# Attention heads in pairs and in a written order, with projections between their steps

## The chip, the cores and the metric

One Trainium2 chip, one NeuronCore of it. The time is device time in microseconds of one execution; a kernel's time is the median of several runs. All times of the trace count from the span's start.

The engines are TensorE (PE; PEld are its weight loads), VectorE (DVE), ScalarE (ACT), GpSimd (POOL) and SyncE (SP), which issues DMAs.

## The reference

Two models stand one behind the other on one sequence of 256 tokens, d_model 1024, all in float32.

The first has two layers on the sequence `x` and a context of 256 tokens `xc`, with modulated norms: a SwiGLU (`ffn1`, d_ff 2816), a mixer of gated convolution, pooling over four windows and neighbourhood attention (eight heads of 64; in layer 0 the context's own attention too), an output projection, and a second SwiGLU. The second has two layers (`hybrid_layer`): one input projection feeds sliding-window attention with sinks (A), stick-breaking attention (B) and block attention (C), each with eight heads of 64; three gated branches are merged, and a SwiGLU with a causal convolution follows.

```
def rms_norm(x, g):
    xf = x.astype(jnp.float32)
    y = xf * lax.rsqrt(jnp.mean(xf * xf, axis=-1, keepdims=True) + RMS_EPS)
    return (y * g.astype(jnp.float32)).astype(x.dtype)

def mod_norm(x, m, i, g):
    return rms_norm(x, g) * (1 + m[:, 3 * i + 1, None]) + m[:, 3 * i, None]
...
        s = jnp.concatenate([s_loc.reshape(B, NA_HEADS, nj, NA_QC, n_loc), s_ctx], axis=-1)
        p = jax.nn.softmax(s, axis=-1).astype(v.dtype)
...
        remain = lax.cumsum(log_one_minus, axis=3, reverse=True) - log_one_minus
        w = jnp.where(past, jnp.exp(log_beta + remain), 0.0)
        return jnp.einsum('bhqk,bkhd->bqhd', w.astype(v.dtype), v)
```

## The kernel before

Activations lie transposed, 128 channels by tokens, in eight tiles (`KT`) for 1024 channels; `n` is 512 where both sequences go through a stage, else 256. A projection (`project`, L149) multiplies weights of a chunk (256 columns by 1024 rows, loaded by `weights`, L109) with these tiles. Each product of float32 operands is done as three products of high and low parts (`mm3`, L139); `split` (L105) makes the parts: ScalarE copies the high part (L106), VectorE subtracts it for the low part (L107). The matmul proper is L133, for projections; in a page its operands are `whi`/`wlo` (weights) and `hhi`/`hlo`, `xhi`/`xlo`, `xg`, `h`, `ghi`/`glo` (activations).

`stats` (L198) gives the root mean square of the normalisation: squares on ScalarE and sums on VectorE (L168), column sums by TensorE with `ones` (`sums`, L178), the power on POOL (L186, `rsqrt`), and `spread` (L189), which turns the four columns by TensorE to all partitions (L193) and copies them (L195). The pair `(0, 0)` says at which `tick` of the projections the two steps come: a tick comes after half of a projection and at its end. A few products on the unnormalised tiles `xhi`/`xlo` run meanwhile; `normed` (L239) then makes the normalised tiles, with a product, an affine operation and a split.

`mix1` (L637) is the mixer of layers 0 and 1. It projects all queries, keys and values, then runs the heads in pairs, with two queries' halves a pair (`attn1`, L601): scores of both heads (L612), softmax on VectorE and ScalarE, transposition of the weights by TensorE (`pt`, L633), values (`o`, L710). Each head has 64 channels, so its scores run on half of the array's rows and its values on half of its columns. The masks of a pair of heads (`bias1`, L593) come by a DMA of POOL's queue and are subtracted on POOL (L598). The gated convolution and the pooling are projected between and after the pairs.

`layer2` (L903) does the same in two layers: the chunks of A, B and C are projected, each group followed by its four pairs of heads (`pair2` L778, `softmax2` L787, `stick2` L808, `pv2` L830; scores L784, transposes L802, stick-breaking sums L821 to L824, values L834 and L836); then twelve chunks of gates, the branches and the ffn.

What sets the order: except where `self.chain` is set, a scheduler puts ready instructions of each engine in an order of its own, and queues and pools of tiles bound what is ready. `mm` (L131) chains matmuls one behind the other only with `self.chain` on. The attentions' matmuls don't go through `mm`, and are not chained.

Of the kernel before, what the change touches and what calls it, by code (L numbers as in the profile page):

```python
# [16 lines left out]
KT = 8  # L17
# [7 lines left out]
WINDOWS = (2, 4, 8, 16)  # L25

# [29 lines left out]
class Kernel:  # L56
# [17 lines left out]
    def chunks():  # L74
# [6 lines left out]
        def mix(l):  # L81
            return [("w_in", l, c) for c in (4, 5, 6, 7, 8, 9, 3, 2, 0, 1)] + [("w_out", l, c) for c in range(4)]
# [48 lines left out]
    def mm(self, *a, **k):  # L131

        i = self.nc.tensor.matmul(*a, **k)  # L133
        if self.chain:
            if self.chained is not None:
                self.after(i, self.chained)
            self.chained = i

# [10 lines left out]
    def project(self, w, width, cols, ops, n):  # L149
        banks = [self.bank("mm") for _ in cols]  # L150
        k = len(ops)
        for i in range(k):
            for ps, c in zip(banks, cols):
                self.mm3(ps[:, :n], self.w_at(w, i, width, c), ops[i], i == 0, i == k - 1)
            if i in (k // 2 - 1, k - 1):
                self.tick()
        return banks

    def project_tok(self, w, width, c0, ops, tts):
        banks = [self.bank("mm") for _ in tts]  # L160
        k = len(ops)
        for ps, tt in zip(banks, tts):
            for i in range(k):
                a = tuple(o[:, tt * 128:tt * 128 + 128] for o in ops[i])
                self.mm3(ps[:, :256], a, self.w_at(w, i, width, c0, 256), i == 0, i == k - 1)
        return banks
# [55 lines left out]
    def modnorm(self, l, i, n, nd):  # L222
# [370 lines left out]
    def bias1(self, l, h):  # L593
        nc = self.nc
        a = self.act(name="tb")
        tb = a[:, :384].rearrange("p (a b) -> p a b", b=64)
        self.after(nc.gpsimd.dma_start(tb, self.t["rpb"][l, h]), self.power)
# [3 lines left out]
    def attn1(self, q, k, tbs):  # L601
# [5 lines left out]
        pts = [self.ptp.tile([128, 4, 256], F32, tag="ptw", name="ptw") for _ in range(2)]  # L607
        for qt in range(2):
            scs = [self.bank("sc") for _ in range(2)]
            for a, sc in enumerate(scs):  # L610
                r = slice(64 * a, 64 * a + 64)
                nc.tensor.matmul(sc[:, :nk], q[r, c0 + qt * 128:c0 + qt * 128 + 128], k[r, c0:c0 + nk], start=True, stop=True)  # L612
            for a, sc in enumerate(scs):
                s = self.swp.tile([128, 512], F32, tag="s", name="s")
                nmx = self.sp.tile([128, 2], F32, tag="nmx", name="nmx")
                if ctx:
                    nc.vector.tensor_reduce(nmx[:, 1:2], sc[:, :256], axis=AX.X, op=ALU.min)
                    ss = self.sp.tile([128, 1], F32, tag="ss", name="ss")
                    self.tabled(nc.scalar.activation(s[:, :256], sc[:, :256], AF.Exp, bias=nmx[:, 1:2], scale=-1.0, accum_out=ss))
                    nc.vector.reciprocal(ss, ss)  # L620
                    nc.vector.tensor_scalar_mul(s[:, :256], s[:, :256], ss)
                else:
                    e0 = 2 - 2 * qt
                    nc.vector.tensor_tensor_reduce(
                        out=s[:, :256], in0=sc[:, :256], in1=tbs[a][0][:, e0:e0 + 4, :].rearrange("p a b -> p (a b)"), scale=1.0, scalar=HUGE,
                        op0=ALU.add, op1=ALU.min, accum_out=nmx[:, 0:1])
                    nc.vector.tensor_tensor_reduce(
                        out=s[:, 256:], in0=sc[:, 256:], in1=self.zeros.to_broadcast([128, 256]), scale=1.0, scalar=nmx[:, 0:1],
                        op0=ALU.add, op1=ALU.min, accum_out=nmx[:, 1:2])
                    self.softmax_tail(s, 512, nmx[:, 1:2])  # L630
                pp = self.bank("pt")
                for kt in range(nk // 128):
                    nc.tensor.transpose(pp[:, kt * 128:kt * 128 + 128], s[:, kt * 128:kt * 128 + 128], self.ident)  # L633
                nc.scalar.activation(pts[a][:, :nk // 128, qt * 128:qt * 128 + 128], pp[:, :nk].rearrange("p (k q) -> p k q", q=128), AF.Copy)
        return pts

    def mix1(self, l, fill=()):  # L637
# [25 lines left out]
        if not last:  # L663
            for ps in self.project(self.weights("w_in", l, 5), 256, (0, 128), sl(n1), n1):
                q = self.act(name="q")
                nc.scalar.activation(q[:, :n1], ps[:, :n1], AF.Copy, scale=-0.125)
                Q.append(q)
        for c in (6, 7):
            for ps in self.project(self.weights("w_in", l, c), 256, (0, 128), sl(512), 512):
# [3 lines left out]
        for c in (8, 9):  # L673
            w = self.weights("w_in", l, c)
            for tt, ps in enumerate(self.project_tok(w, 256, 0, ops, range(4))):
                nc.scalar.activation(V[tt][:, (c - 8) * 256:(c - 8) * 256 + 256], ps[:, :256], AF.Copy)

        def sums(m):
            v, su3 = Z[m]
            self.pool_sums(v, ns, m, su3)  # L680
            nc.gpsimd.tensor_tensor(su3, su3, self.invcnt[:, m, None, :].to_broadcast([128, ns, 256]), op=ALU.mult)
            nc.gpsimd.tensor_tensor(su3, su3, v[:, :ns, 8:264], op=ALU.subtract)

        tbs = [[self.bias1(l, h) for h in range(2)]]
        SU, Z = [], []
        for m, ps in enumerate(self.project(self.weights("w_in", l, 3), 256, (0, 128), sl(n1), n1)):
            v = self.zp.tile([128, 2, 272], F32, tag="z", name="z")
            nc.gpsimd.memset(v[:, :, 0:8], 0.0)
            nc.gpsimd.memset(v[:, :, 264:272], 0.0)
            nc.scalar.activation(v[:, :ns, 8:264], ps[:, :n1].rearrange("p (s t) -> p s t", t=256), AF.Copy)  # L690
# [212 lines left out]
    def layer2(self, L):  # L903
# [68 lines left out]
        if L == 0:  # L972
            close()
# [294 lines left out]
```

## Time and profile before

| | us |
|---|---|
| median of 3 runs | 2617.03 (2615.76 to 2618.78) |
| profiled execution | 2616.04 |
| its span | 2614.3 |
| PE busy | 2576.7 (99%) |
| DVE busy | 1761.1 (67%) |
| ACT busy | 1172.8 (45%) |
| POOL busy | 72.1 (3%) |

The span is the time from the first to the last instruction of the core. A busy share says in how much of it the engine worked, not whether what it did was needed or at the best rate: a TensorE that computes one half of its array at a time is busy all the same. The chain of work that ended last has TensorE in 78% of it, with the projections' L133 alone 72%.

Timelines list start and duration of groups of equal instructions of one line. One float32 matmul of attention makes two records, a transposition one; a projection's matmul of split operands makes one. Times of matmuls' ends are modelled, so the steps between starts are the better measure of pace.

### The profile page before, as it was taken

How to read it: one execution, taken by the hardware profiler on the slowest of the kernel's cores; microseconds unless marked ns; L12 is line 12 of the kernel's file. 1: busy time of each engine (PE TensorE's matmuls, PEld its weight loads, DVE VectorE, ACT ScalarE, POOL GpSimd, SP SyncE). 2: the span in 40 equal slices, each digit the busy share in tenths (PEclk: the TensorE clock that was granted, in tenths of full speed). 3: DMA queues.
4: the chain of work that ended last, by engine and by line, in shares of the span. 5: the costliest groups of instructions: out<-in, count | busy, mean ns of one | idle time of the engine just before them, and what ended most of it. 6: DMA issues, size and time to landing. Idle time of an engine off the chain costs nothing.

```text
span 2614.3 us, 39984 instructions
## 1 busy us (share of the span) xinstructions
PE 2576.7 (99%) x16156; PEld 2241.0 (86%) x16156; DVE 1761.1 (67%) x3309; ACT 1172.8 (45%) x2120; POOL 72.1 (3%) x93
## 2 busy tenths in 40 slices
PE   8999999999999999999999999999999999999998
PEld 5888888668888888888887799988999998899998
DVE  6877755557867758765354665677579856758984
ACT  5222234545222234222234554457556645755664
POOL 0000002200000000000003000000000000000000
PEclk9999999999999999999999999999999999999999
DMA  7545533112545533444233254632454463245544
GB/s 289 214 161 192 175 128 115 55 52 106 192 160 191 176 122 144 175 163 155 73 127 119 95 187 166 203 137 101 162 190 170 169 211 133 98 164 192 178 163 145
DMA packets 64857, 401.69 MB, mean 154 GB/s; under 512 B 7456, under 2 KB 7584, under 8 KB 26656
## 3 DMA queue, kind: packets, MB, share of 16 engines
q1 hardware_dynamic: 63360, 395.20, 42.9%
q0 software_dynamic: 1024, 3.15, 0.4%
q8 instruction: 127, 2.08, 0.3%
q10 hardware_dynamic: 288, 0.79, 0.1%
q14 instruction: 58, 0.48, 0.1%
HBM read 398.06 MB, written 1.05 MB: 153 GB/s over the span
## 4 chain that ended last, share of the span: by engine, by line
PE 78%; DVE 3%; ACT 2%; issue 1%; POOL 0%; POOLq 0%; DVEq 0%; ACTq 0%
PE mm L133 72%; PE sc L612 1%; PE sc L784 1%; PE o L834 1%; PE o L710 1%; PE pt L633 1%; DVE wlo L107 1%; ACT whi L106 1%; ACT t L845 1%; PE pt L802 1%; POOL r L186 0%; PE o L836 0%; PE pt L180 0%; DVE n L242 0%; PE sc L193 0%
## 5 line engine op out<-in xcount | busy, mean ns | idle before, releaser
L106 ACT ACTIVATE whi<-raw 128x1024 fp32r<-128x1024 f32 (+2 forms) x704 | 621.0, 925 | 545.0 <-issue 271.5
L107 DVE TENSOR_TENSOR wlo<-raw,whi 128x1024 fp32r<-128x1024 f32 (+2 forms) x704 | 730.4, 1066 | 166.2 <-ACT whi L106 165.2
L133 PE MATMUL mm<-hlo,whi 128*128 128x512 f32 (+1 forms) x1520 | 556.0, 366 | 2.9 <-DVE hlo L107 2.8
L133 PE MATMUL mm<-hhi,wlo 128*128 128x512 f32 (+1 forms) x1520 | 555.8, 366 | 0.1
L133 PE MATMUL mm<-hhi,whi 128*128 128x512 f32 (+1 forms) x1520 | 553.4, 366 | 0.0
L133 PEld LDWEIGHTS mm<-hlo,whi 128*128 128x128 f32 x1520 | 285.4, 188 | 55.8 <-DVE hlo L107 3.4
L133 PEld LDWEIGHTS mm<-hhi,whi 128*128 128x128 f32 x1520 | 285.6, 188 | 52.6 <-issue 2.3
L133 PEld LDWEIGHTS mm<-hhi,wlo 128*128 128x128 f32 x1520 | 285.5, 188 | 52.4 <-issue 2.2
L133 PE MATMUL mm<-xg,whi 128*128 128x256 f32 x1600 | 294.4, 284 | 0.0
L517 ACT ACTIVATE t<-mm 128x512 f32<-128x512 f32 (+1 forms) x82 | 44.9, 547 | 522.1 <-PE mm L133 522.1
L133 PEld LDWEIGHTS mm<-xg,whi 128*128 128x128 f32 x1600 | 246.4, 188 | 5.1 <-issue 4.2
L133 PE MATMUL mm<-h,whi 128*128 128x256 f32 x1280 | 227.4, 280 | 0.3
L133 PE MATMUL mm<-xg,wlo 128*128 128x256 f32 x800 | 227.2, 284 | 0.0
L133 PE MATMUL mm<-ghi,whi 128*128 128x512 f32 x528 | 208.1, 394 | 0.0
L133 PE MATMUL mm<-ghi,wlo 128*128 128x512 f32 x528 | 207.9, 394 | 0.0
L133 PE MATMUL mm<-glo,whi 128*128 128x512 f32 x528 | 207.9, 394 | 0.0
L133 PEld LDWEIGHTS mm<-h,whi 128*128 128x128 f32 x1280 | 196.1, 188 | 1.2 <-DVE h L107 1.1
L434 DVE CUSTOM_DVE_ANT_0 junk<-raw,cb,par 128x1024 bf16<-128x1024 f32 x128 | 164.0, 1281 | 48.4 <-DMA raw<-in_w_mod 48.4
L416 DVE SCALAR_TENSOR_TENSOR x<-mm,m,x 128x256 f32<-128x256 f32 x128 | 56.0, 479 | 191.6 <-PE mm L133 191.0
L133 PE MATMUL mm<-h,wlo 128*128 128x256 f32 x640 | 179.0, 280 | 0.0
L434 DVE CUSTOM_DVE_ANT_0 raw<-raw,cb,par 128x1024 f32<-128x1024 f32 x128 | 164.4, 1284 | 3.6
L133 PEld LDWEIGHTS mm<-xg,wlo 128*128 128x128 f32 x800 | 151.2, 189 | 4.6 <-issue 4.1
(269 smaller groups left out, 4041.7 us busy)
## 6 DMA issues: line engine op xcount, KB each, us to landing
raw<-in_ffn_w_in SPq DMA_DIRECT2D x86, 1024.0 KB, 4.8
raw<-in_w_in SPq DMA_DIRECT2D x74, 1024.0 KB, 4.8
raw<-in_w_mod SPq DMA_DIRECT2D x64, 1024.0 KB, 4.8
raw<-in_ffn_w_out SPq DMA_DIRECT2D x64, 704.0 KB, 4.1
raw<-in_w_up SPq DMA_DIRECT2D x44, 1024.0 KB, 4.8
raw<-in_w_down SPq DMA_DIRECT2D x32, 704.0 KB, 4.1
raw<-in_w_out SPq DMA_DIRECT2D x16, 1024.0 KB, 4.8
raw<-in_w_branch SPq DMA_DIRECT2D x12, 1024.0 KB, 4.8
```

The source lines that it names most:

```text
L106: self.nc.scalar.activation(hi, src, AF.Copy)
L107: self.nc.vector.tensor_sub(lo, src, hi.bitcast(F32))
L133: i = self.nc.tensor.matmul(*a, **k)
L416: self.nc.vector.scalar_tensor_tensor(out=self.X[m][:, c], in0=ps[:, c], scalar=self.mod(l, i, m, r), in1=self.X[m][:, c], op0=ALU.mult, o ...
L434: nc.vector.tensor_tensor_reduce(out=w if r else self.junk, in0=w, in1=self.cb[:, r, :], scale=1.0, scalar=self.par["b_mod"][:, c:c + 1], ...
L517: self.tabled(nc.scalar.activation(g[:, :n], pa[:, :n], AF.Silu))
L612: nc.tensor.matmul(sc[:, :nk], q[r, c0 + qt * 128:c0 + qt * 128 + 128], k[r, c0:c0 + nk], start=True, stop=True)
L633: nc.tensor.transpose(pp[:, kt * 128:kt * 128 + 128], s[:, kt * 128:kt * 128 + 128], self.ident)
L710: nc.tensor.matmul(o[64 * a:64 * a + 64, :256], v[:, h * 64:h * 64 + 64], pts[a][:, kt, :], start=(kt == 0), stop=(kt == len(vs) - 1), til ...
L784: self.nc.tensor.matmul(sc[:, o:o + n], a[r, ca:ca + 128], b[r, cb:cb + n], start=True, stop=True)
L802: nc.tensor.transpose(pp[:, (qt + i) * 128 if qt == 0 or i == 0 else 256:((qt + i) * 128 if qt == 0 or i == 0 else 256) + 128], s[:, a + i ...
L834: nc.tensor.matmul(o[64 * a:64 * a + 64, 0:256], v[0][:, cols[a]:cols[a] + 64], pts[a][:, 0:256], start=True, stop=False, tile_position=(0 ...
```

## The change

Attention is cut into units: two heads, and in `mix1` one half of the queries. A unit has three steps: scores, `weights` (transposes, or the stick-breaking sums), values. `weave` issues a unit's scores, then projections for a given time, the unit before's `weights`, more projections, that unit's values, and goes on. `ROOM1` and `ROOM2` hold the times; a projection reports its time as columns times products over 2200. The projections come from a generator (`stream`), in which the chunks' order is written; what isn't used up goes behind the units. While `written()` is on, all of TensorE's instructions are chained through `mm` and `flip`.

Beside it: `stats` of modulated norms and of layer 2's ffn spread at tick 2; `normed` makes each tile by two products with the root mean square, two high parts on ScalarE and two differences of 256 columns; masks are subtracted by VectorE (`masked1`), for the first pair of heads ahead of the units, later beside them; chunk order in `w_in`; `w_out` takes the mixer's parts in the order 4, 5, 6, 7, 2, 3, 0, 1; the ffn of layer 2 has three early chunks; pools of weights and of `rb` in part 2 have two tiles instead of three, scores have four.

```
+ROOM1 = (((3.6, 2.4), (2.2, 1.4)), ((3.3, 2.2),) * 2)
+ROOM2 = (4.6, 3.0)
...
-            return [("w_in", l, c) for c in (4, 5, 6, 7, 8, 9, 3, 2, 0, 1)] + [("w_out", l, c) for c in range(4)]
+            return [("w_in", l, c) for c in ((4, 6, 8, 5, 7, 9), (4, 5, 6, 8, 7, 9))[l] + (3, 2, 0, 1)] + [("w_out", l, c) for c in range(4)]
...
+    def flip(self, dst, src):
+        self.link(self.nc.tensor.transpose(dst, src, self.ident))
...
+    def fill(self, us):
+        self.owed += us
+        while self.owed > 0 and self.stream is not None:
+            try:
+                self.owed -= next(self.stream)
+            except StopIteration:
+                self.stream = None
+
+    def weave(self, units, stream, lead):
+        self.stream, self.owed = stream, 0.0
+        with self.written():
+            self.fill(lead)
+            for u in range(len(units) + 1):
+                if u < len(units):
+                    while not units[u].ready():
+                        self.fill(0.1 - self.owed)
+                    units[u].scores()
+                a, b = units[u - 1 if u else 0].room
+                self.fill(a)
+                if u:
+                    units[u - 1].weights()
+                    self.fill(b)
+                    units[u - 1].values()
+            self.fill(1e6)
...
-        self.stats(self.X, n, (0, 0))
+        self.stats(self.X, n, (0, 2))
...
-                nc.vector.tensor_tensor(t[:, :n], self.X[kt][:, :n], self.rb[:, :n], op=ALU.mult)
+                hi, lo = self.act(F32R, "hhi"), self.act(F32R, "hlo")
                 for r in segs:
                     c = slice(r * 256, r * 256 + 256)
-                    if r and kt % 2:
-                        nc.vector.tensor_scalar(t[:, c], t[:, c], self.mod(l, i + 1, kt, r), self.mod(l, i, kt, r), op0=ALU.mult, op1=ALU.add)
-                    else:
-                        nc.scalar.activation(t[:, c], t[:, c], AF.Identity, bias=self.mod(l, i, kt, r), scale=self.mod(l, i + 1, kt, r))
-                hi, lo = self.act(F32R, "hhi"), self.act(F32R, "hlo")
-                self.split(hi[:, :n], lo[:, :n], t[:, :n])
+                    sh = self.mod(l, i, kt, r)
+                    nc.vector.scalar_tensor_tensor(out=t[:, c], in0=self.X[kt][:, c], scalar=self.mod(l, i + 1, kt, r), in1=self.rb[:, c], op0=ALU.mult, op1=ALU.mult)
+                    nc.scalar.activation(hi[:, c], t[:, c], AF.Identity, bias=sh)
+                    nc.vector.scalar_tensor_tensor(out=lo[:, c], in0=t[:, c], scalar=sh, in1=hi[:, c].bitcast(F32), op0=ALU.add, op1=ALU.subtract)
...
-        nc.gpsimd.tensor_tensor(tb, self.colmask[:, None, :].to_broadcast([128, 6, 64]), tb, op=ALU.subtract)
+    def masked1(self, tb):
+        self.nc.vector.tensor_tensor(tb, self.colmask[:, None, :].to_broadcast([128, 6, 64]), tb, op=ALU.subtract)
...
+        self.weave([unit(p, ctx, qt) for p in range(4) for ctx in ((False,) if last else (False, True)) for qt in range(2)], stream(), 1.4)
...
+        self.weave([f(m) for f in (unit_a, unit_b, unit_c) for m in range(4)], stream(), 6.0)
...
-        self.stats(X, 256, (0, 0))
+        self.stats(X, 256, (0, 2))
```

Three places of the order, before (first fence of each) and after. TensorE in the mixer of layer 1 (`mm` projections, `sc` scores, `pt` transposes, `o` values), where the first pairs of heads begin, before:

```order
L612 MATMUL sc<-k,q 128x512
L633 MATMUL pt<-ident,s 128x128 x4
L612 MATMUL sc<-k,q 128x512
L633 MATMUL pt<-ident,s 128x128 x4
L612 MATMUL sc<-k,q 128x512
L633 MATMUL pt<-ident,s 128x128 x4
L612 MATMUL sc<-k,q 128x512
L633 MATMUL pt<-ident,s 128x128 x4
L710 MATMUL o<-ptw,v 64x256
```

And after, further along in the same attention:

```order
L138 MATMUL mm<-hhi,whi 128x256
L138 MATMUL mm<-hlo,whi 128x256
L138 MATMUL mm<-hhi,wlo 128x256
L138 MATMUL o<-ptw,v 64x256 x8
L138 MATMUL sc<-k,q 128x512 x2
L138 MATMUL mm<-hhi,whi 128x256
L138 MATMUL mm<-hlo,whi 128x256
L138 MATMUL mm<-hhi,wlo 128x256
```

Scores of single heads stood between transposes of others; now a pair's two scores stand together, behind all eight value matmuls of the unit before, and projections go between the steps.

TensorE in layer 2's first layer, among the units of C (`qk` queries and keys, `xg` the projections' tiles), before:

```order
L784 MATMUL sc<-qk 128x128
L802 MATMUL pt<-ident,s 128x128
L784 MATMUL sc<-qk 128x256
L133 MATMUL mm<-xg,whi 128x256
L802 MATMUL pt<-ident,s 128x128 x2
L133 MATMUL mm<-xg,whi 128x256
L834 MATMUL o<-ptw,v 64x256
L784 MATMUL sc<-qk 128x128
L784 MATMUL sc<-qk 128x256
L834 MATMUL o<-ptw,v 64x256
L836 MATMUL o<-ptw,v 64x128 x2
```

And after:

```order
L138 MATMUL mm<-xg,whi 128x256 x2
L138 MATMUL mm<-xg,wlo 128x256
L138 MATMUL o<-ptw,v 64x256 x2
L138 MATMUL o<-ptw,v 64x128 x2
L138 MATMUL sc<-qk 128x128 x2
L138 MATMUL sc<-qk 128x256 x2
L138 MATMUL mm<-xg,whi 128x256 x2
L138 MATMUL mm<-xg,wlo 128x256
```

Scores and values of one unit were cut by transposes of another and by single projections; now both heads' scores, and both heads' values, are whole groups.

TensorE at the start of the ffn behind the first mixer (`pt<-ones,t` the column sums, `sc<-ident,r` the spread), before:

```order
L180 MATMUL pt<-ones,t 128x1 x4
L133 MATMUL mm<-xhi,whi 128x258
L133 MATMUL mm<-xlo,whi 128x258
L133 MATMUL mm<-xhi,wlo 128x258
L133 MATMUL mm<-xhi,whi 128x258
L133 MATMUL mm<-xlo,whi 128x258
L133 MATMUL mm<-xhi,wlo 128x258
L133 MATMUL mm<-xhi,whi 128x258
L193 MATMUL sc<-ident,r 128x128 x4
```

And after:

```order
L237 MATMUL pt<-ones,t 128x1 x4
L138 MATMUL mm<-xhi,whi 128x258
L138 MATMUL mm<-xlo,whi 128x258
L138 MATMUL mm<-xhi,wlo 128x258
L138 MATMUL mm<-xhi,whi 128x258
L138 MATMUL mm<-xlo,whi 128x258
L138 MATMUL mm<-xhi,wlo 128x258
L138 MATMUL mm<-xhi,whi 128x258
L138 MATMUL mm<-xlo,whi 128x258
L138 MATMUL mm<-xhi,wlo 128x258
L250 MATMUL sc<-ident,r 128x128 x4
```

Seven products stood between the column sums and the spread; now there are nine.

## Rows read from the trace of the kernel before

**Rows 1.** Page, busy time (share of the span) and instructions of each engine.

```profile
PE 2576.7 (99%) x16156; PEld 2241.0 (86%) x16156; DVE 1761.1 (67%) x3309; ACT 1172.8 (45%) x2120; POOL 72.1 (3%) x93
```

**Rows 2.** Windows of projections: length; PE, PEld, DVE, ACT, POOL busy (records); clock, DMA, GB/s.

```profile
200.00:300.00 100.00, 100.00 (x433) 80.90 (x432) 77.73 (x117) 26.82 (x36) 0.00 (x0) 1.00 0.52 185
2000.00:2100.00 100.00, 100.00 (x851) 100.00 (x850) 79.52 (x137) 63.79 (x106) 0.00 (x0) 1.00 0.51 178
```

**Rows 3.** Windows with attention, projections of L133 alone.

```profile
480.00:546.00 66.00, 15.07 (x51) 8.39 (x50) 1.00 0.07 23
1424.00:1465.00 41.00, 7.51 (x51) 6.13 (x49) 1.00 0.18 61
1716.00:1840.00 124.00, 79.06 (x597) 72.72 (x596) 1.00 0.32 113
2171.00:2297.00 126.00, 79.69 (x605) 73.55 (x604) 1.00 0.32 113
```

**Rows 4.** Timeline, mixer 0, both heads' scores: start, us, line, shape.

```profile
480.42 0.39 PE L133 MATMUL mm<-hhi,wlo 128*128 128x512 f32 x1
480.74 1.13 PE L612 MATMUL sc<-k,q 64*128 64x512 f32 x4
481.80 0.50 PE L133 MATMUL mm<-hhi,whi 128*128 128x512 f32 x1
482.14 0.39 PE L133 MATMUL mm<-hlo,whi 128*128 128x512 f32 x1
```

**Rows 5.** Timeline, mixer 1, scores of one head alone.

```profile
1430.89 1.12 PE L612 MATMUL sc<-k,q 64*128 64x512 f32 x2
```

**Rows 6.** Timeline, mixer 1, values of one unit.

```profile
1455.06 0.65 PE L710 MATMUL o<-ptw,v 128*64 128x256 f32 x2
...
1456.65 1.94 PE L710 MATMUL o<-ptw,v 128*64 128x256 f32 x14
```

**Rows 7.** Timeline, mixer 0, eight transposes, and a context pair's scores.

```profile
505.16 1.10 PE L633 MATMUL pt<-ident,s 128*128 128x128 f32 x8
506.01 0.48 PE L133 MATMUL mm<-hlo,whi 128*128 128x512 f32 x1
...
507.89 0.77 PE L612 MATMUL sc<-k,q 64*128 64x256 f32 x4
```

**Rows 8.** Timeline, layer 2, scores of both heads of a unit.

```profile
1762.87 0.92 PE L784 MATMUL sc<-qk 64*128 64x256 f32 x8
1763.73 0.50 PE L133 MATMUL mm<-xg,whi 128*128 128x256 f32 x2
```

**Rows 9.** Window with attention in layer 2, all engines.

```profile
1716.00:1840.00 124.00, 121.69 (x901) 102.32 (x900) 84.28 (x249) 81.42 (x190) 0.00 (x0) 1.00 0.32 113
```

**Rows 10.** TensorE's waits: total us, times, longest.

```profile
PE sc L193 <- POOL r L186: 5.2, 8, 0.9
...
PE o L834 <- ACT ptw L827: 3.0, 3, 1.5
PE mm L133 <- DVE hlo L107: 2.8, 1, 2.8
...
PE mm L133 <- DVE mlo L107: 1.4, 2, 0.8
```

**Rows 11.** VectorE's operations by form: count, busy us, mean ns.

```profile
L107 DVE TENSOR_TENSOR hlo<-n,hhi 128x512 fp32r<-128x512 f32 x32 | 23.7, 760 | 0.0
L242 DVE TENSOR_TENSOR n<-x,rb 128x512 f32<-128x512 f32 x32 | 22.7, 735 | 0.0
...
L246 DVE TENSOR_SCALAR n<-n,m,m 128x256 f32<-128x256 f32 x16 | 7.9, 495 | 0.0
...
L398 DVE SCALAR_TENSOR_TENSOR hlo<-n,m,hhi 128x256 fp32r<-128x256 f32 x16 | 6.9, 479 | 0.0
```

**Rows 12.** Timeline, VectorE and POOL at mixer 1's masks.

```profile
1378.62 1.48 DVE L107 TENSOR_TENSOR hlo<-n,hhi 128x512 fp32r<-128x512 f32 x1
...
1374.24 5.30 POOL L598 TENSOR_TENSOR tb<-k,tb 128x384 f32<-128x384 f32 x4 [1.10 <-DMA tb<-in_rpb]
```

More of the change, by code (lines that the diff above doesn't have):

```diff
@@ L606, in attn1 @@
         c0 = 256 if ctx else 0
[L607 to L634, printed above, removed]
@@ L662, in mix1, with head @@
         normed()
[L663 to L669, printed above, removed]
+        def head(c):
+            banks = yield from self.projected(self.weights("w_in", l, c), 256, (0, 128), sl(512), 512)
+            for ps in banks:
                 k = self.act(name="k")
@@ new lines, in stream @@
+        def stream():
+            if not last:
+                banks = yield from self.projected(self.weights("w_in", l, 5), 256, (0, 128), sl(n1), n1)
+                for ps in banks:
+                    q = self.act(name="q")
+                    nc.scalar.activation(q[:, :n1], ps[:, :n1], AF.Copy, scale=-0.125)
+                    Q.append(q)
+            yield from head(7)
+            yield from toks(9)
+            yield from pooled()
+            yield from conv()
+        SU, mix = [], [None] * 8
@@ new lines, in mix1, with unit, scores, weights @@
+        pair = lambda: (self.act(F32R, "mhi"), self.act(F32R, "mlo"))
+        tbs = [[self.bias1(l, h) for h in range(2)]]
+        self.drain(head(6))
+        self.drain(toks(8))
+        for tb, _ in tbs[0]:
+            self.masked1(tb)
+        PT = {}
+        def unit(p, ctx, qt):
+            def scores():
+                if qt == 0 and not ctx and p < 3:
+                    tbs.append([self.bias1(l, 2 * p + 2 + a) for a in range(2)])
+                u.S = self.scores1(Q[p], K[p], None if ctx else tbs[p], qt)
+                if qt and not ctx:
+                    self.slots.free(*(a for _, a in tbs[p]))
+                    if p < 3:
+                        for tb, _ in tbs[p + 1]:
+                            self.masked1(tb)
+                if qt and ctx != last:
+                    self.slots.free(Q[p], K[p])
+            def weights():
+                if qt == 0:
+                    PT[p, ctx] = [self.ptp.tile([128, 4, 256], F32, tag="ptw", name="ptw") for _ in range(2)]
+                self.turned1(u.S, PT[p, ctx], 2 if ctx else 4, qt)
+            def values():
+                if qt == 0:
+                    return
+                if not ctx:
+                    mix[4 + p] = pair()
@@ L713, in mix1 @@
                 self.split(mix[4 + p][0][:, c], mix[4 + p][1][:, c], o[:, :256])
-                if not ctx:
-                    self.slots.free(*(a for _, a in tbs[p]))
-            self.slots.free(Q[p], K[p])
+            u = SimpleNamespace(scores=scores, weights=weights, values=values, ready=lambda: len(K) > p and len(Q) > p,
+                                room=ROOM1[l][ctx])
+            return u
+        self.weave([unit(p, ctx, qt) for p in range(4) for ctx in ((False,) if last else (False, True)) for qt in range(2)], stream(), 1.4)
@@ L776, in pool_sums, with scores2 @@
         add(dst[hi], s8[hi, :ns, 4:260], s8[hi, :ns, 12:268])
-    def pair2(self, one, first, second):
+    def scores2(self, first, second):
         scs = [self.bank("sc") for _ in range(2)]
@@ L1001, in layer2, with unit, scores, weights @@
-        self.slots.free(*ops)
+        ropek(pk, kv[:, :256])
+        A.K = [kv[:, :256]] * 4
+        A.V = [kv[:, 256:384], kv[:, 384:512]]
+        O, G, gates = [], [], []
+        mk = self.masks
+        def unit(a, m, need, sides, one, turn, cols, end=None):
+            def scores():
+                u.S = [one(sc, h) for h, sc in enumerate(self.scores2(*sides()))]
+            def weights():
+                u.P = [turn(s) for s in u.S]
+            def values():
+                O.append(self.pv2(u.P, a.V, cols))
+                if m == 3:
+                    self.slots.free(*a.held)
+                    if end:
+                        end()
+            u = SimpleNamespace(scores=scores, weights=weights, values=values, ready=lambda: len(a.K) > m and len(need) > m, room=ROOM2)
+            return u
@@ L1036, in layer2 @@
         pre = self.xg(g)
-        self.stats(X, 256, (0, 0))
+        self.stats(X, 256, (0, 2))
         ops = []
-        early = [self.project(self.weights("w_up", L, j), 256, (0, 128), halves(pre), 256) for j in range(2)]
-        rb = self.rb[:, :256]
         def normed(kt):
```

386 lines of the change are left out of this document (218 added, 168 removed).

## The prediction

> **What bounds the kernel now.** I read the page first, then stretches of the timeline, then the list of waits. TensorE is busy 2576.7 of 2614.3 us [rows 1], so what can be won is TensorE's own time, or the 38 us in which it stands. The projections set the pace: in a stretch with nothing else 433 matmuls of 512 columns start in 100 us, 231 ns each, and 851 of 256 columns, 117.5 ns each, at a granted clock of 1.00 [rows 2]. The diff keeps their number and shapes, so their time stays. What isn't projection stands in four stretches with attention. The projections there number 51, 51, 597 and 605 [rows 3]; at 231.6, 117.6, 117.6 and 117.6 ns they need 11.8, 6.0, 70.2 and 71.1 us. The rest of the stretches' 66, 41, 124 and 126 us is 54.2, 35.0, 53.8 and 54.9 us, 198 us in all: the attentions with everything that they cost TensorE, its waits included.
>
> **What the attentions could cost.** A head uses half of the array, and two heads' matmuls on the two halves can run at once. Where both stand side by side, their four records take 1.13 us [rows 4]; where one stands alone between transposes, its two records take 1.12 us [rows 5]. A broken pair of scores therefore costs a whole 1.06 us more (start to start). Values are the same: two records alone 0.65 us, and the fourteen left after that 1.94 us [rows 6], of which the first head's start is paid for twice. In before the scheduler often sends the first head as soon as its tile is free: the first order fence of mix1(1) shows four lone scores in a row, the second fence lone 128- and 256-column scores and a lone value.
>
> The new order emits each pair whole, with projections around it. The price of such a step is read from before, where it occurs now and then:
> - Pair of 512-key scores: from the projection at 480.42 to the one at 482.14 are 1.72 us [rows 4]; less two projections at 0.2316, 1.26 us. Of this 1.06 is the pair and 0.2 the change to half-array tiles and back.
> - Pair of 256-key scores: 0.77 us as recorded [rows 7], some 0.07 of it overlap with the next, and 0.1 to 0.2 for the change: 0.83.
> - Eight transposes: 0.85 us from 505.16 to the projection at 506.01 [rows 7], 0.106 each, no change of tiles.
> - Values of two heads and four key tiles: the fourteen records start to start take about 1.88 and hold one lone head, so sixteen in pairs take the same, 1.88, and 0.08 to 0.1 more for the change: 1.96. With two key tiles 1.10.
> - Layer 2, scores of two heads (eight records): 1762.87 to 1763.73 are 0.86 us [rows 8], with the 0.2 for the change of tiles 1.05; values 0.88 by the share of columns; six transposes 0.65; for a stick-breaking unit sixteen records of 128 columns instead, 1.8.
>
> Per pair of heads mix1(0) needs 2 x (1.26 + 0.87) + 1.96 for the neighbourhood and 2 x (0.83 + 0.44) + 1.10 for the context, 9.85; four pairs 39.4 us. mix1(1) has no context queries: 4 x 6.22 = 24.9. A layer of part 2: eight softmax units at 1.05 + 0.65 + 0.88 = 2.59 and four stick units at 3.75 are 35.7 us, twice 71.4. Sum 135.7. The gain by order is 198 - 136 = 62, say **-62 us**, if TensorE never waits for a softmax.
>
> A change of tiles has its own price: 480.42 to 480.74 is 0.32 us for a matmul of 0.2316, 0.09 more [rows 4]. Counted in the two orders, the four stretches of before hold 251 runs of instructions in one mode of tiles, the new order 140, so about 111 x 0.1 = 11 of the 62 us are these. [...]
>
> **Waits of the new order.** All of TensorE's instructions in these stages are chained now: a transposition that comes before its softmax is done holds every projection behind it, where before the scheduler's order put ready work first. There are 48 units (16, 8, 12, 12). After a unit's scores some 3.6 us of projections stand before the previous unit's transposes, and some 2.4 more before its values (the assumed room of 2.2 to 4.6 and 1.4 to 3.0 us in the tables). One unit back means that a softmax has a whole unit, 6 to 10 us. A 512-key softmax on before's rows is a chain of about 4 to 5 us for two heads on VectorE and ScalarE, so it fits when those engines are not behind. They are not behind on average: in the first layer-2 stretch VectorE works 84.3 and ScalarE 81.4 of 124 us [rows 9], and with TensorE's part 18 us shorter it would be 84.3 of 106, 80%. The units are uneven, though, and before itself waits 3.0 us for a copied weight tile in three places [rows 10]. What a written order adds isn't shown; bounds are 0 and, at 0.8 us (half of the longest such wait, 1.5) for each of 48 units, 40. I take 0.2 us a unit, **+10 us**, nearer to the rows: three waits of 1.0 on average among layer 2's 24 units are 0.13 a unit.
>
> **Smaller parts.** The root mean squares: TensorE stands 5.2 us in eight places for POOL's power before the spreading transposes [rows 10]; the third fence shows nine products instead of seven between the sums and the spread at 128x258, and more at the other places, about 1 us of cover more. I count **-5 us**; the bounds are 0 and -5.2. What the later spread costs: after it only 48 early products (5.7 us) stand before the first normalised tile is wanted, against 64 to 74 before. VectorE made a tile with a product of 0.735, a difference of 0.760 and, for one of two segments on every second tile, an affine of 0.495, 1.74 us; now it makes four operations of 0.479 [rows 11], 1.92 us, while TensorE uses a tile up in 6 x 0.2316 = 1.39 us. So over eight tiles VectorE falls 8 x 0.53 = 4.2 us behind, from a lead of 5.7 less the latency of the first tile (about 2 us) and less VectorE's own backlog of weight splits. I put 2.5 us on each of the three places with 512 columns that show no such wait today; mix1(1), which waits 2.8 us for the same operation [rows 10], stays: **+7.5 us**, with 0 and +15 as bounds.
>
> The masks leave POOL for VectorE: sixteen operations of 128x384, each between the 0.479 of 256 columns and the 0.735 of 512 [rows 11], some 9 to 10 us, hidden behind the projections before the first softmax. What they free is seen at 1378: while POOL works 5.30 us on four masks, VectorE's difference of 512 columns takes 1.48 us where its mean is 0.760 [rows 11, 12]. [...] I leave it inside the bounds of the term above.
>
> The output projection takes the attention's part first and the gated convolution's last, where TensorE waits 1.4 us for the split of the mixed tiles today [rows 10]; with the transposes of A's values moved behind a projection I count **-2 us** for both. Layer 2's third early chunk moves sixty-four products from one operand to another and no time. The tiles taken from the pools (two instead of three for transposed weights, four instead of two for scores) cost nothing but waits that are counted above.
>
> **Sum.** -62 + 10 - 5 + 7.5 - 2 = -51.5 us against the profiled execution's 2616.0 (span 2614.3 and 1.7 around it): 2564.5. The median of the three runs is 1.0 us above that execution, so 2565; I say **2564 us**. Its own range, from the bounds of the small terms and 0 to 20 of waits, is 2545 to 2580.
>
> **Rivals.**
> - VectorE and ScalarE become the bound in layer 2. Where the four rotated chunks stand beside stick-breaking units, the third of the 106 us is dense: at 110% of an engine instead of 80%, 3.5 us a layer are late, and with TensorE chained each late piece also holds the projections, so two or three times that, some 8 us a layer. For it: 84.3 us of work [rows 9] don't shrink. Against: the projections between the units spread it. Time: 2564 + 16 = 2580. Chance 0.2.
> - The pairs don't join, because something between the two heads' matmuls still makes them wait. Then only mode changes (11), the spread (5) and TensorE's attention waits go, and the terms of +17 stay: about -20, 2597. For it: it isn't shown with a chained order. Against: [rows 4] and [rows 8] show it in the same program. Chance 0.08.
> - Slower than before: TensorE waits in its fixed order at every transposition for a late softmax. The place is the 48 units, the price is the wait per unit; it decides from 62 / 48, 1.3 us above the 0.2 taken, about 1.5 us a unit. At 2 us a unit the attentions cost 96 - 10 more: 2650. For it: before waits up to 1.5 us for a weight tile even with ready work first [rows 10]. Against: a unit's room. Chance 0.05.
> - The change gives nothing: waits eat the gain, within 0.2% (5.2 us, about what a measurement of this kernel can tell from none). Chance 0.03.
>
> **How the numbers follow.** Forecast 0.64, the first rival 0.20, the second 0.08, slower 0.05, none 0.03. Range 2540 to 2599: it holds the forecast, the first rival and most of the second. Faster 0.92, same 0.03, slower 0.05.
>
> **What would show it.** In the changed profile: every half-array score and value in groups of 4, 8 or 16 records, none of 2 (order term right); TensorE's waits at transposes and values under 15 us together (else the first or third rival); the wait for POOL's power gone, and a wait of TensorE for the normalised differences of about 2.5 us at each of three places (spread terms); no operation of VectorE's there at double its mean (masks). The forecast is wrong if the attentions' rest comes out above 160 us.

## The result, and the profile after

The changed kernel takes 2569.84 us (median of 4 runs, 2569.36 to 2570.26) against 2617.82 of before beside it: 48.0 us less, ratio 0.9818 with the interval 0.9801 to 0.9835. The forecast was 2564 and its range 2540 to 2599. The profiled execution has a span of 2568.4 us at a mean granted clock of 0.995 (before 2614.3 at 0.999).

The page's first part, then TensorE's waits (total us, times, longest), which answer to [rows 1] and [rows 10]:

```profile
PE 2529.4 (98%) x16156; PEld 2228.4 (87%) x16156; DVE 1771.0 (69%) x3377; ACT 1156.0 (45%) x2096; POOL 50.4 (2%) x77
```

```profile
PE o L138 <- ACT ptw L923: 11.3, 4, 4.2
...
PE mm L138 <- DVE t L1178: 5.1, 2, 2.6
...
PE o L138 <- ACT ptw L694: 1.6, 1, 1.6
PE mm L138 <- ACT hhi L304: 1.6, 2, 1.1
...
PE sc L250 <- POOL r L243: 0.6, 1, 0.6
```

TensorE is busy 47 us less at the same number of matmuls. POOL's power is gone from its waits but for 0.6 us, and so are the low parts of the normalised and of the mixed tiles; the normalised tiles' high parts (`hhi`) stand with 1.6. In their place are waits of 11.3 us in four places, for the exponentiated weight tiles at the end of a stick-breaking unit (`ptw`, L923), and of 5.1 us in two, for a product of VectorE (L1178) in layer 2's ffn.

The pairs are whole, but for one unit's values in the second mixer, which stand as 2 and 14 records. The timeline of the first mixer shows values of sixteen records and scores of four:

```profile
487.13 1.95 PE L138 MATMUL o<-ptw,v 128*64 128x256 f32 x16
489.01 0.70 PE L138 MATMUL sc<-k,q 64*128 64x256 f32 x4
...
501.36 1.13 PE L138 MATMUL sc<-k,q 64*128 64x512 f32 x4
```

Sixteen value records take 1.95 us, where [rows 6] needed 0.65 and 1.94 for the same work, and two heads' scores 1.13 us with no lone ones left [rows 4, 5].

Cut at the column sums that open each normalisation, the program has these stages (us; the rest of it differs by 0.1 in all):

| stage | before | after | |
|---|---|---|---|
| first mixer | 218.3 | 202.1 | -16.2 |
| its ffn, and layer 1's first | 739.0 | 738.7 | -0.3 |
| second mixer | 146.1 | 132.8 | -13.3 |
| its ffn | 192.5 | 192.6 | +0.1 |
| part 2, layer 0: attentions, branches | 264.8 | 254.1 | -10.7 |
| its ffn | 191.9 | 195.4 | +3.5 |
| part 2, layer 1: attentions, branches | 263.7 | 251.8 | -11.9 |
| its ffn | 187.9 | 190.7 | +2.8 |

So the gain, 52.1 us, lies where the units are, and part 2's two ffn give 6.3 of it back. What waits in part 2 is seen at the first two B units. TensorE's timeline, then VectorE's of the same time, then windows of all engines (length; PE, PEld, DVE, ACT, POOL busy; clock; DMA share; GB/s):

```profile
1740.79 1.95 PE L138 MATMUL pt<-nl,k 128*128 128x128 f32 x16
...
1745.29 0.28 PE L138 MATMUL mm<-xg,wlo 128*128 128x256 f32 x1
1749.75 2.01 PE L138 MATMUL o<-ptw,v 128*64 128x256 f32 x8 [4.18 <-ACT ptw L923]
1751.68 1.65 PE L138 MATMUL sc<-qk 64*128 64x256 f32 x8
1753.26 0.79 PE L138 MATMUL mm<-xg,whi 128*128 128x256 f32 x2
```

```profile
1745.97 1.23 DVE L112 TENSOR_TENSOR wlo<-raw,whi 128x1024 fp32r<-128x1024 f32 x1
1747.12 0.42 DVE L944 TENSOR_TENSOR qk<-qk,t 128x256 f32<-128x256 f32 x1
1747.45 1.22 DVE L112 TENSOR_TENSOR wlo<-raw,whi 128x1024 fp32r<-128x1024 f32 x1
1748.59 1.01 DVE L921 TENSOR_TENSOR s<-s,pt 128x384 f32<-128x384 f32 x2
```

```profile
1745.00:1749.70 4.70, 0.56 (x5) 0.36 (x3) 4.60 (x8) 2.42 (x4) 0.00 (x0) 0.93 0.06 7
1749.70:1752.00 2.30, 2.25 (x10) 1.40 (x12) 0.00 (x0) 0.67 (x2) 0.00 (x0) 0.50 0.88 303
1752.00:1754.00 2.00, 2.00 (x11) 1.60 (x10) 1.06 (x3) 0.28 (x2) 0.00 (x0) 0.50 0.38 160
1754.00:1756.00 2.00, 2.00 (x12) 2.00 (x11) 0.13 (x1) 2.00 (x6) 0.00 (x0) 0.52 0.00 0
1756.00:1758.00 2.00, 2.00 (x19) 2.00 (x19) 1.95 (x4) 1.92 (x6) 0.00 (x0) 1.00 0.04 8
```

The values at 1749.75 wait 4.18 us. What they want is an exponential of a sum (L921) that VectorE does at 1748.59, although TensorE's sums for it began at 1740.79 and took 1.95: VectorE first does the rotations of a chunk (L944 ends one) and two weight splits of 1.23 us. Then the granted clock is 0.50 until 1756: the eight value records take 2.01 us where 0.87 is usual, the scores 1.65 where 0.92 is. Half the clock for 6.3 us makes the wait of 4.2 us 3.1 us dearer, an estimate that takes half of that time as lost. Layer 1 has the same wait (4.21 us from 2193.8), with the clock at 0.50 for 5.0 us of work behind it, 2.5 us dearer by the same estimate.

The ffn has the like, a wait of 2.49 us before the first product on normalised tiles. TensorE, then VectorE:

```profile
1937.36 0.28 PE L138 MATMUL mm<-xg,wlo 128*128 128x256 f32 x1
1940.13 0.67 PE L138 MATMUL mm<-h,whi 128*128 128x256 f32 x2 [2.49 <-DVE t L1178]
```

```profile
1937.98 0.88 DVE L1199 SCALAR_TENSOR_TENSOR t<-t,par 128x255 f32<-128x255 f32 x2
1938.77 0.88 DVE L1200 SCALAR_TENSOR_TENSOR t<-t,par 128x254 f32<-128x254 f32 x2
1939.56 0.76 DVE L1178 TENSOR_TENSOR t<-mm,rb 128x256 f32<-128x256 f32 x2
```

It is not these tiles that are late. The product `t<-mm` at 1939.56 empties the banks (PSUM tiles that matmuls write) of the second early chunk; the third early chunk holds the other pair of the four banks, so nothing else can start. In the 3.4 us behind it the clock is 0.53:

```profile
1940.00:1943.40 3.40, 3.27 (x16) 3.30 (x17) 3.39 (x10) 2.32 (x5) 0.00 (x0) 0.53 0.63 267
```

### The profile page after: what moved, and what is told of

Read it like the earlier page. It is cut to its first block, busy times and chain, and to the rows that moved or that the text cites. A ratio compares the mean times of both kernels' runs of the same rounds, so it can differ in the third digit from the quotient of the medians.

```text
span 2568.4 us, 39952 instructions
## 1 busy us (share of the span) xinstructions
PE 2529.4 (98%) x16156; PEld 2228.4 (87%) x16156; DVE 1771.0 (69%) x3377; ACT 1156.0 (45%) x2096; POOL 50.4 (2%) x77
## 3 DMA queue, kind: packets, MB, share of 16 engines
q8 instruction: 127, 2.08, 0.3%
## 5 line engine op out<-in xcount | busy, mean ns | idle before, releaser
L138 PE MATMUL mm<-xg,whi 128*128 128x256 f32 x1664 | 303.9, 284 | 0.0
L138 PEld LDWEIGHTS mm<-xg,whi 128*128 128x128 f32 x1664 | 256.3, 190 | 5.6 <-issue 5.1
L138 PE MATMUL mm<-xg,wlo 128*128 128x256 f32 x832 | 234.1, 281 | 0.0
L138 PE MATMUL mm<-h,whi 128*128 128x256 f32 x1216 | 218.6, 283 | 5.1 <-DVE t L1178 5.1
L138 PEld LDWEIGHTS mm<-h,whi 128*128 128x128 f32 x1216 | 188.9, 191 | 5.5 <-ACT t L1202 5.5
L138 PE MATMUL mm<-h,wlo 128*128 128x256 f32 x608 | 171.6, 283 | 0.0
L138 PEld LDWEIGHTS mm<-xg,wlo 128*128 128x128 f32 x832 | 157.4, 189 | 0.0
```

The costliest lines, as they stand in the source:

```text
L138: self.link(self.nc.tensor.matmul(*a, **k))
```

## The experiments

All times are medians against the changed kernel's 2569.8; each variant ran beside the kernel before (2616.8 to 2618.3), and the ratio is to that.

**free_order.** The chain off.

```
-        self.chain, self.chained = True, None
+        self.chain, self.chained = False, None
```

> The changed kernel with the chaining switched off in the attention stages; units, steps and the written order of issue stay. Theory: two heads' scores and values come together because each unit now issues them together, a step late, and the chain only fixes what the scheduler would do anyway; it runs within 8 us of the changed kernel's 2569.8, 2562 to 2578, and no lone scores come back. Rival: the chain is what keeps the pairs whole; lone heads come back and with them about half of the gain or more, 2595 or above.

2563.46 us, ratio 0.9790 (0.9775 to 0.9804): the theory. The scores take 45.0 us of the four stages (start to start), 44.0 with the chain and 71.8 before, and no lone ones come back, so the pairs come from issuing both heads in one step. TensorE, its projections no longer held by the chain, waits 2.2 us at most at the B units where the chain waits 4.2, and the half clock behind that lasts 3.4 us instead of 6.8. The chain costs 6 us here; it does not make the gain.

**unwoven.** All rooms 0.0; a unit is issued only once its branch's values are projected too.

```
-ROOM1 = (((3.6, 2.4), (2.2, 1.4)), ((3.3, 2.2),) * 2)
-ROOM2 = (4.6, 3.0)
+ROOM1 = (((0.0, 0.0),) * 2,) * 2
+ROOM2 = (0.0, 0.0)
```

> The changed kernel with all rooms at 0: pairs stay whole and chained, but no projections stand between a unit's steps, apart from those a unit needs itself. Theory: the room hides the softmax chains; without it TensorE waits in each of the 48 units for VectorE and ScalarE, some 2 to 3 us each, 100 to 150 us in all, and the time is 2650 to 2730, slower than before. Rival: the gain comes from pairs alone, and the one-unit lag hides the softmax without projections: 2565 to 2590.

2659.91 us, ratio 1.0159 (1.0144 to 1.0174), slower than before as the theory had it. The longest of TensorE's waits:

```profile
PE o L138 <- ACT ptw L899: 17.1, 17, 1.8
PE o L138 <- ACT ptw L924: 13.2, 10, 2.9
PE o L138 <- ACT ptw L694: 8.0, 13, 1.4
PE sc L138 <- DVE s L912: 8.0, 2, 4.0
PE sc L138 <- DVE nmx L884: 6.4, 3, 3.6
```

The scores' pairs are whole here too. So whole pairs in a fixed order, without room, lose 42 us against before; the rooms are worth 90 us, because TensorE stands at scores, transposes and values when no projection is there. A part of the 90 us is the clock: in these stages it is 0.50 in eight stretches with 32.9 us of TensorE's work, by estimate some 16 us lost where the changed kernel loses 5.6.

**room_b.** More room ahead of the B units' values.

```
-            u = SimpleNamespace(scores=scores, weights=weights, values=values, ..., room=ROOM2)
+            u = SimpleNamespace(scores=scores, weights=weights, values=values, ..., room=ROOM2 if a is not B else (4.6, 8.0))
```

> The changed kernel with 8.0 instead of 3.0 us of projections ahead of the values of the stick-breaking units (B). Theory: the waits of 4.3 and 1.6 us at the values of the first two B units go, and with them the half clock that follows the longer one (granted 0.50 to 0.52 for about 6 us, some 3 us lost); two layers x 9 us: 2552 to 2556. Rival: VectorE and ScalarE are the bound in that stretch, so the wait moves to another unit: 2565 to 2572.

2557.90 us, ratio 0.9769 (0.9755 to 0.9784): 11.9 us of the 14 to 18 that the theory had. The waits at the B units are gone, and these stand in their place, for the parts of the weights of the next chunks; behind those of layer 1 the clock is at half, as the window shows:

```profile
PE mm L138 <- ACT whi L111: 2.5, 2, 1.3
PE mm L138 <- DVE wlo L112: 2.1, 3, 0.9
```

```profile
2206.80:2210.30 3.50, 3.50 (x19) 3.50 (x18) 3.10 (x5) 2.58 (x5) 0.00 (x0) 0.51 0.65 218
```

So the rival is partly right: of 11.3 us of waits that left, 4.6 came back as waits for weights' parts, and some 1.7 us at half clock came with them in layer 1; layer 0 has none.

**two_early.** Two early chunks in layer 2's ffn.

```
-        early.append(up(2, pre))
...
-            src = early[0] if j == 0 else plain(early[j]) if j < 3 else up(j, ops)
+            src = early[0] if j == 0 else plain(early[j]) if j < 2 else up(j, ops)
```

> The changed kernel with two early chunks in layer 2's ffn, as before, the spread still at tick 2. Theory: the wait of 2.7 us in each of the two ffn, for the emptying of the second early chunk's banks behind VectorE's normalisation, comes from the third early chunk, and the half clock behind it costs 1.5 more; without it 2560 to 2563. Rival: the third chunk hides the later spread, so a wait for the normalised tiles takes its place: 2567 to 2575.

2566.48 us, ratio 0.9801 (0.9785 to 0.9817): 3.4 us, between the two. The wait for banks, 2.5 and 2.6 us, is gone in both ffn, and so is the half clock behind it (195.4 to 193.6, 190.7 to 188.9); 0.9 us of waiting for weights stands in its place. The third early chunk is the cause of 3.6 of the 6.3 us that the two ffn lost.

**spread_at_0.** Both `stats` at tick 0.

```
-        self.stats(self.X, n, (0, 2))
+        self.stats(self.X, n, (0, 0))
...
-        self.stats(X, 256, (0, 2))
+        self.stats(X, 256, (0, 0))
```

> The changed kernel with the root mean squares spread at tick 0 again, in the modulated norms and in layer 2's ffn. Theory (the forecast's term of -5): TensorE waits again some 0.5 to 1.0 us for POOL's power in seven or eight places and nothing else changes: 2573 to 2576. Rival: what the early spread costs, it gives back at the normalised tiles, which are ready sooner (waits of 1.3, 0.6 and 0.6 us in the modulated norms and 2.7 us in each ffn of layer 2 shrink): 2562 to 2570.

2565.41 us, ratio 0.9804 (0.9789 to 0.9818): the rival. POOL's waits return and the time still falls by 4.4 us:

```profile
PE sc L250 <- POOL r L243: 4.1, 6, 0.9
...
PE mm L138 <- DVE t L1178: 1.3, 1, 1.3
```

Layer 2's ffn take 193.3 and 188.5 us instead of 195.4 and 190.7; in the five stages with modulated norms the sum changes by 0.4 us. The later spread pays nothing in these and costs 4.3 us in layer 2's ffn.

**old_normed.** Normalised tiles made as before.

```
+                nc.vector.tensor_tensor(t[:, :n], self.X[kt][:, :n], self.rb[:, :n], op=ALU.mult)
...
+                hi, lo = self.act(F32R, "hhi"), self.act(F32R, "hlo")
+                self.split(hi[:, :n], lo[:, :n], t[:, :n])
```

> The changed kernel with the normalised tiles made in before's way (product of 512 columns, affine, split). Theory (the forecast's term of +7.5, 2.5 us at each of three places, for the slower VectorE work of the new way): 2560 to 2565. Rival, from the trace after, where only 1.3, 0.6 and 0.6 us of waits for these tiles stand: the new way costs next to nothing or gains: 2568 to 2574.

2570.11 us, ratio 0.9822 (0.9808 to 0.9837): the rival; no difference. The new way of normalising is neither a cost nor a gain.

**pool_masks.** Masks on POOL again, issued where the changed kernel issues their DMA.

```
+        self.nc.gpsimd.tensor_tensor(tb, self.colmask[:, None, :].to_broadcast([128, 6, 64]), tb, op=ALU.subtract)
...
     def masked1(self, tb):
-        self.nc.vector.tensor_tensor(tb, self.colmask[:, None, :].to_broadcast([128, 6, 64]), tb, op=ALU.subtract)
+        pass
```

> The changed kernel with the masks subtracted by POOL again, right behind their DMA. Theory: POOL's work slows VectorE's normalisation in the second mixer as before and the wait there grows from 1.3 to about 2.8 us, with late masks a little more in the units: 2571 to 2574. Rival: the masks lie beside other work on either engine: 2568.5 to 2571.

2582.98 us, ratio 0.9872 (0.9856 to 0.9889): 13.1 us slower, where the theory had 1 to 4. The first mixer's start, VectorE (with POOL's masks), POOL, TensorE, and VectorE of the changed kernel:

```profile
413.41 7.59 DVE L303 SCALAR_TENSOR_TENSOR n<-x,m,rb 128x256 f32<-128x256 f32 x5
```

```profile
413.12 2.42 POOL L652 TENSOR_TENSOR tb<-k,tb 128x384 f32<-128x384 f32 x2
...
416.07 3.85 POOL L652 TENSOR_TENSOR tb<-k,tb 128x384 f32<-128x384 f32 x4
```

```profile
416.41 0.73 PE L138 MATMUL mm<-hhi,whi 128*128 128x512 f32 x2 [0.15 <-ACT hhi L304]
421.85 0.80 PE L138 MATMUL mm<-hlo,whi 128*128 128x512 f32 x1 [4.70 <-DVE hlo L305]
```

```profile
412.82 2.08 DVE L303 SCALAR_TENSOR_TENSOR n<-x,m,rb 128x256 f32<-128x256 f32 x5
```

Five products of VectorE take 7.59 us while POOL works, and 2.08 without it; TensorE stands 4.70 us. What in POOL's work holds the products up isn't shown. Behind the 4.70 us the granted clock is 0.50 until 426, with projections 0.43 us apart (422.44 to 422.87) where 0.23 is usual [rows 2], by estimate some 2.1 us more. In the second mixer TensorE waits 1.1 us for the differences and 3.4 for weights' parts, with 3.4 us at half clock behind them. Stage by stage it is 7.4 us in the first mixer and 6.7 in the second.

**masks_alone.** The same move in the kernel before, and nothing else.

```
-        nc.gpsimd.tensor_tensor(tb, self.colmask[:, None, :].to_broadcast([128, 6, 64]), tb, op=ALU.subtract)
+        nc.vector.tensor_tensor(tb, self.colmask[:, None, :].to_broadcast([128, 6, 64]), tb, op=ALU.subtract)
```

> The kernel before with one line changed: the masks are subtracted by VectorE instead of POOL. Theory: in before the masks collide only with the end of the second mixer's normalisation (VectorE's differences at 1.48 instead of 0.76 us), so 2 of the 2.8 us wait there go: 2613 to 2616. Rival: the move alone is worth the 13 us by which the changed kernel gets slower when its masks go back to POOL: 2603 to 2606.

2630.09 us, ratio 1.0045 (1.0028 to 1.0062): both theories fall, it is 12 us slower. VectorE, POOL and TensorE in the first mixer, and a window behind the wait:

```profile
500.01 0.56 DVE L598 TENSOR_TENSOR tb<-k,tb 128x384 f32<-128x384 f32 x1 [8.65 <-DMA tb<-in_rpb]
```

```profile
496.19 1.26 POOL L682 TENSOR_TENSOR su<-su,z 128x512 f32<-128x512 f32 x1
497.40 0.59 POOL L597 DMA_DIRECT2D tb<-in_rpb  x1
```

```profile
501.50 1.08 PE L633 MATMUL pt<-ident,s 128*128 128x128 f32 x4 [7.73 <-DVE ss L620]
```

```profile
501.50:510.60 9.10, 9.10 (x29) 4.47 (x30) 3.29 (x11) 2.28 (x7) 0.00 (x0) 0.50 0.01 2
```

The next pair's mask waits for its bias table, whose DMA (L597) POOL issues only after the pooling sums that stand in its queue; VectorE waits 8.65 us with the mask at its head, the softmax behind it, and TensorE 7.73. Half the clock behind it, 0.50 for 9.1 us, makes this by estimate 4.6 us dearer; the stage is 15.5 us longer than in before. There the same wait stands on POOL, with no softmax behind it. In the second mixer TensorE's wait of 2.8 us for the differences [rows 10] is gone, and the stage is 1.1 us shorter (146.1 to 145.0), the part that the theory saw. The changed kernel issues the DMAs a unit ahead of the mask, and in the first mixer all eight are issued by 423, long before the sums at 500.5.

**lone_heads.** Pairs broken up: one projection between two heads' scores, values of one head first (in the mixers; in part 2 the values stay).

```
+            if a == 0:
+                self.fill(0.1 - self.owed)
...
-                for kt, v in enumerate(vs):
-                    for a in range(2):
+                for a in range(2):
+                    for kt, v in enumerate(vs):
```

> The changed kernel with its pairs broken on purpose: one projection's products stand between the two heads' scores, and the values of the first head all come before those of the second. Theory: two heads on two halves of the array run at once, so a broken pair costs the time of a whole head more: scores 16 x 1.26, 8 x 0.75 and 24 x 1.06 us, values 8 x 1.9, 4 x 0.9 and 24 x 0.8 us, about 90 us, 2640 to 2665, slower than before. Rival: matmuls of one head follow each other as fast as those of two, and only the additional changes of tiles are paid, 0.2 us in 48 units: 2575 to 2590.

2623.51 us, ratio 1.0022 (1.0013 to 1.0031): 53.7 us slower than the changed kernel, and slower than before, so the theory, at 60% of its size. The timeline:

```profile
480.99 1.12 PE L138 MATMUL sc<-k,q 64*128 64x512 f32 x2
482.04 0.39 PE L138 MATMUL mm<-whi,hhi 128*128 128x256 f32 x1
...
482.59 1.12 PE L138 MATMUL sc<-k,q 64*128 64x512 f32 x2
...
500.23 2.86 PE L138 MATMUL o<-ptw,v 128*64 128x256 f32 x16
```

A lone score takes 1.12 us, as in [rows 5]; start to start the scores of the four stages take 86.5 us instead of 44.0. Sixteen value records with one head behind the other take 2.86 us, not twice 1.95; that part of the two heads' work still overlaps is read from these two figures alone. The expectation had doubled them, and had counted part 2's values, which weren't broken.

**room_b_flush.** room_b, and the second early chunk emptied together with the first.

```
-        early[0] = plain(early[0])
+        early = [plain(b) for b in early]
```

> Room of 8.0 us ahead of the values of the B units, and in layer 2's ffn the second early chunk is taken out of its banks together with the first, ahead of the normalisation. Theory: the waits for the second chunk's banks (2.7 us and about 1.5 at half the clock, twice) go, so 8 us below the 2557.9 of the room alone: 2548 to 2552. Rival: VectorE has the same work in front of the normalised tiles and the wait moves there: 2556 to 2559.

2554.33 us, ratio 0.9762 (0.9748 to 0.9777): 3.6 us below room_b, between the two. Waits of 0.8 and 0.6 us remain in the first ffn, of 1.0 and 0.6 in the second.

**best_chained, best_free.** Room 6.0 for B, 2.0 more ahead of the first values of a stage, layer 2's ffn as before; without the chain in the second.

```
+                    self.fill(b + (2.0 if u == 1 else 0.0))
```

> The changed kernel with 6.0 us ahead of the B units' values, 2.0 us more ahead of each stage's first values, and layer 2's ffn as before (two early chunks, spread at tick 0). Theory: the waits at the first B units and at the first unit of the first mixer go, with the half clock behind them (20 to 22 us with the ffn's 6): 2547 to 2552. Rival: at this room VectorE and ScalarE are still behind with the weights' parts: 2553 to 2558.

> As best_chained, with the chain off. Theory: the 6 us that the changed kernel gained without its chain were the shorter waits at the B units; with the room in place nothing is left to gain: within 2 us of best_chained. Rival: the fixed order costs by itself in every stage: 4 us or more below best_chained.

2555.02 us (ratio 0.9760, 0.9746 to 0.9775) and 2553.90 (0.9756, 0.9742 to 0.9771). best_free holds its theory, 1.1 us below the first: their waits are the same, so the fixed order adds none, and the one stage that differs (part 2's first ffn, 195.1 and 193.6) has a stretch at half clock in best_chained alone. best_chained misses its theory by 3 us and lies in its rival's range: layer 2's ffn, as before by their code, still take 195.1 and 191.2 us, not 191.9 and 187.9, because each waits 2.2 us for weights' parts, with 3.4 us at half clock behind. TensorE's longest waits of best_free have them:

```profile
PE mm L138 <- DVE wlo L112: 6.2, 4, 2.2
```

So the gains of two_early and of spread_at_0 in these ffn don't add up. In nearly every variant VectorE is what these ffn wait for, for the banks, the tiles or the parts. In best_chained's first ffn it is busy without a gap until it makes the awaited part at 1931.73, with steps of the convolution just ahead of it; why the parts come later than in before is left open. These and room_b_flush are the best versions run, 15 to 16 us below the changed kernel and not to be told apart.

## Why the prediction was right, and where its steps failed

The time lay in the range, 5.8 us above the forecast, and most of the gain came from where it was put. By its steps:

- *Order, -62, and waits of the written order, +10*: together -52; the four stages give -52.1, of which some 6 us are other waits that went (1.1 twice for the spread, 1.7 at the second mixer's normalisation, 2.4 before the output projections). Leaves -46. The order's gain holds: breaking the pairs costs 54 us, and taking the room away 90; start to start, scores, transposes with the stick-breaking sums, and values take 124.9 us instead of 179.0. The share of fewer changes of tiles, 11 of the 62, wasn't tried apart from the pairs, since lone_heads adds changes too. The waits were mis-sized: from start to start they are 13.7 us (1.7, twice 4.3 to 4.4, twice 1.6), in five places instead of 48, and the half clock behind the two long ones is by estimate 5.6 more, which no term had. Without both the order gives 46 + 13.7 + 5.6 = 65, an estimate: with the spread back at tick 0 the mixers aren't longer (202.3 and 132.3 us), so 2 of the 6 us may be the order's. The place is the one of the first rival: rotated chunks beside the first B units, some 9 us a layer with the clock, where it had said 8 beyond the 10. room_b shows that more room takes most of it away.
- *Spread, -5*: the waits for POOL went (5.2 to 0.6 us), but they are worth nothing: with the spread at tick 0 the kernel is 4.4 us faster. The step took a wait that goes for time that goes.
- *Later spread and slower normalisation, +7.5 at three places*: failed. None of the three places waits (the 1.6 us for `hhi` are 1.1 in the second mixer and 0.45 in its ffn), and old_normed gives the same time. VectorE's five products in a run take 2.08 us above, 0.42 each and not the 0.479 of the single row, so four operations are 1.7 us a tile and the lead of the early products suffices.
- *Third early chunk, no time*: failed, +6.3 us in part 2's ffn; each of two edits takes part of it away, two early chunks 3.6 and the spread at tick 0 4.3, but with both together, in best_chained, none is gone, so its cause is settled only as far as VectorE being late there. That +7.5 and +6.3 are near each other is chance.
- *Masks, hidden, with no term of their own*: held. The second mixer's wait for its normalised tiles fell from 2.8 to 1.1 us, and in masks_alone, where nothing else moved, it went. What the prediction didn't see is the price of not moving them: in the new order masks on POOL cost 13.1 us, since they come beside the normalisation in both mixers, where it had one late difference in before (1.48 us where 0.76 was the mean [rows 11, 12]).
- *Output projection, -2*: the waits for the mixed tiles' parts are gone from the list (1.4 and 0.5 us). It wasn't tried alone.
- *Slower than before* has not come; its mechanism is unwoven's, +1.6%, and what keeps it away is the room.

## What to carry to other kernels

When two instructions can run on halves of an array, issue both in one step and put other work between the steps, not between the two: here two heads' scores took 1.13 us together and one head's alone 1.12. Price a wait on TensorE with what comes behind it (here 6.3 us at a clock of 0.50 behind 4.2 us of standing), and look for it where the densest work of the other engines stands, not as an average over units. And a move to another engine is decided by what queues behind the moved instruction: the same masks on VectorE lost 12 us in the kernel before, behind a late DMA, and saved 13 in the changed one, where the DMAs come early and five products of the normalisation took 7.59 us beside POOL's masks instead of 2.08.

## What the runs showed of the hardware that was not expected

TensorE's granted clock fell to half after waits that the trace of before hardly has: 0.50 for 6.3 us behind 4.2 us of standing, and 0.53 for 3.4 us behind 2.5 us. Eight value records took 2.01 us in the first of these and 0.87 at a clock of 1.00. The length of a wait alone doesn't tell what follows: in before 2.8 us of standing at 1377 had no such stretch behind it (1.00 from 1376 to 1384), and in two_early the same wait of 4.2 us at the first B unit is followed by half the clock for most of 4.1 us in layer 0 and for all of 5.8 us in layer 1:

```profile
1750.60:1754.70 4.10, 4.04 (x19) 2.74 (x20) 1.02 (x3) 0.92 (x4) 0.00 (x0) 0.59 0.71 250
2196.10:2201.90 5.80, 5.78 (x26) 4.52 (x27) 1.19 (x3) 2.45 (x7) 0.00 (x0) 0.50 0.45 174
```

So a us or two between variants can be the clock's alone, by estimate: half of 6.3 us at 0.51 is lost in layer 0 of the changed kernel, and some 1.7 of 4.1 at 0.59 in two_early. In the changed kernel's stages a clock near half shows only at the end of four waits, of 4.2, 2.5, 4.2 and 2.6 us, and behind them; what sets it off isn't shown.
